# A copy of the first weights at another address, a fixed order for one chunk, and a prepared mean in a two-layer encoder

## The chip, the core and the metric

The kernel runs on one core of a Trainium2 chip. The core has a matmul engine (TensorE, PE in the profile; its weight loads stand apart as PEld), three engines for elementwise work (VectorE, DVE; ScalarE, ACT; GpSimd, POOL), a queue engine (SyncE, SP) and 16 DMA engines. Each engine runs its own instructions in order and waits for the others on semaphores. The metric is the device time of one execution in microseconds (us), the median over several runs of the same kernel.

## The reference

Two encoder layers on 256 tokens of width 2048, with 256 memory tokens beside them. In short:

```python
m = rms_norm(mem, mem_norm)
for i in range(2):
    n = rms_norm(h, attn_norm[i])
    # layer 0: 12 heads of 2-D neighbourhood attention with a bias
    # layer 1: 12 query heads on 4 key heads, normed q and k, rotary positions
    # both: 4 more heads that attend to the memory
    q, k, v, qm = split(n @ w_in[i])
    km, vm = split(m @ w_mem_kv[i])
    h = h + concatenate([mix(q, k, v), memory_attention(qm, km, vm)]) @ w_o[i]
    n = rms_norm(h, mlp_norm[i])
    h = h + square(relu(n @ w_up[i])) @ w_down[i]      # 2048 -> 8192 -> 2048
return rms_norm(h, final_norm)
```

All arrays are float32. The output is 256 x 2048.

## The kernel before

Every large product is made of three matmuls. A float32 operand is split into `hi` (rounded by ACT to the matmul's type) and `lo` (the rest, a subtraction on DVE), and the product sums hi x hi, hi x lo and lo x hi. The function `split` (L399) does this for weights, which come in chunks of 128 x 2048 (1 MB a DMA on SP, tile `raw`), a chunk in two halves (`hf` 0 and 1) of 1024 columns.

Matmuls come in two forms. In the S form (`products`, L306) the weights are the stationary operand, 128 x 128, and the activations stream past them, 256 columns at a time. The projections of queries and keys (`ps_s`) and the up projection of the MLP (`ps_u`) are of this form. In the M form (`m_products`, L289) the activations are stationary and 512 columns of weights stream: values, the output projection and the plain part of the down projection (`ps_m`). The down projection of the other parts (`p1` to `p7`, L913 to L925) also streams 512 columns.

The work is a list of grains (`Grain`, L115) that `run_all` (L343) goes through. A grain has a run (its matmuls) and earlier stages: load, pre and prep (the splits), each called a given number of grains ahead. A scheduler then orders the instructions of each engine from what they depend on and when it believes them ready. Where the program wants an order of its own it says so: `pin` keeps an instruction in the program's order, and `tc.issue_after(x)` lets nothing inside it be issued before `x`. `past` (L702) uses two such rules, one for an ACT and one for a DVE instruction.

Several constants (L39 to L52) shift tiles by some bytes within their rooms, so that what streams and what is loaded as stationary lie at chosen addresses: `STILL_AT` for the S form's weights, `MOVING_AT`, `LAST_AT`, `U_AT`. `ENTRY_AT` (160 bytes) belongs to `entered_half` (L267): where an S chunk follows an M chunk, the first 128 columns of `lo` are put at an address of their own (`Entered`, L101), and the first three matmuls of that chunk begin with `lo`. The tiles `hi` and `lo` are 64 elements longer than a half, which is the room for the shifts.

The MLP's up projection runs in 8 parts of 8 chunks (`up_grains`, L809). Part 0 stands before the down projection; each chunk of parts 1 to 7 stands between two grains of the part before it: down first, up (48 matmuls of 256 columns), down second. That makes a step of some 10 us. ACT and DVE split the weights of the next step meanwhile.

In layer 1 the output projection follows attention closely. `add_o` (L775) puts the chunks of output blocks 0 and 1 into one order, in which the chunk `late`, whose heads are the last to be ready, comes last for both blocks. The last two chunks are marked `behind` (L786): the split of their second half waits for the softmax of the newest head (`box["sm"]`, an exp on ACT and a product on DVE), and the very last chunk multiplies in `last_but_one` (L255), in which the products of its second quarter wait for the newest `av` product. The heads run as three stages each, `attend`, `attend2` (transposes, then the split into `pT`) and `attend3` (`av`, then the split into `cat`), set by `attention` (L492) at given distances in grains.

The end of the kernel is `finish` (L1099), once for each half of the tokens: it adds the last 512 columns to `h`, squares them on ACT, sums the four parts of the mean square, takes the root on POOL (`rstd_of`, L404), scales, and stores.

Of the kernel before, what the change touches and what calls it, by code (L numbers as in the profile page):

```python
# [14 lines left out]
ALU = mybir.AluOpType  # L15
# [36 lines left out]
ENTRY_AT = 160  # L52
# [13 lines left out]
class Work:  # L66


    def __init__(self, kind, src, acts, first, begins, last, start, done):
        self.kind, self.src, self.acts = kind, src, acts  # L70
        self.first, self.begins, self.last, self.start, self.done = first, begins, last, start, done
        self.early = self.behind = False
# [48 lines left out]
def encoder_kernel(ctx: ExitStack, tc: tile.TileContext, t: dict, out: bass.AP):  # L121
# [79 lines left out]
    def halves_of(w):  # L201
# [53 lines left out]
    def last_but_one(w, hi, lo):  # L255

        for i in range(NT):
            m_products(w, w.first, 1, i, hi, lo, False, False)
        with tc.issue_after(box["av"].ins):
            for i in range(NT):  # L260
                m_products(w, w.first + 1, 1, i, hi[:, 512:], lo[:, 512:], False, False)

    def new_half(kind):
        s = slice(STILL_AT // 4, STILL_AT // 4 + HALF) if kind == "S" else slice(0, HALF)
        return tuple(at.ring.tile([P, HALF + 64], F32R, tag=n, bufs=4, name=n)[:, s] for n in ("hi", "lo"))
# [23 lines left out]
    def m_products(w, k0, nk, i, hi, lo, begins, ends, keep_order=False):  # L289

        acts = w.acts
        for j in range(nk):
# [7 lines left out]
            nc.tensor.matmul(w.ps[i], al, hi[:, s], start=False, stop=sp)  # L300
# [5 lines left out]
    def products(ps, acts, k0, nk, hi, lo, keep_order=False):  # L306

        for j in range(nk):
# [7 lines left out]
            for n, (x, part) in enumerate(parts):  # L316
                ins = nc.tensor.matmul(ps, x[:, s], acts[:, k, part], start=k == n == 0,  # L317
# [129 lines left out]
    def attend(qT, kT, bias=None):  # L447
# [16 lines left out]
        for s in range(NT):  # L464
            exp = nc.scalar.activation(sc[:, s, :], src[:, s, :], AF.Exp, bias=nm[:, s : s + 1],
                                       accum_out=sm[:, s : s + 1])
        rs = small.tile([P, NT], F32, tag="rs", name="rs")
        nc.vector.reciprocal(rs, sm)
        for s in range(NT):
            times = nc.vector.tensor_scalar(sc[:, s, :], sc[:, s, :], rs[:, s : s + 1], None, op0=ALU.mult)  # L470
        box["sm"] = exp, times
        return sc

    def attend2(sc):
# [6 lines left out]
        split(pT[:, 0], pT[:, 1], pt)  # L481
        return pT
# [9 lines left out]
    def attention(jobs, at, gap=1, lag=1, rest=0):  # L492


        def step(n, job, prev):
# [3 lines left out]
            elif n == 1:  # L499
                res = attend2(prev)  # L500
            else:
                return attend3(prev, v, head, cat)
# [272 lines left out]
    def add_o(layer):  # L775
        first, second, third, late = 3, 0, 1, 2
        for n in (0, 2):
# [7 lines left out]
            if layer and n == 0:  # L785
                plan[-1].behind = plan[-2].behind = True  # L786
# [22 lines left out]
    def up_grains(layer, part, m):  # L809
# [5 lines left out]
        def prep(hf):  # L815
# [10 lines left out]
            else:  # L826
                own[hf] = half_of_side(own["raw"], hf)

        def run(hf):
# [14 lines left out]
            products(own["ps"], box["hT" if part else "hT0"], hf * (KT // 2), KT // 2, *own.pop(hf), keep_order=part > 0)  # L844
# [254 lines left out]
    def finish(w, i):  # L1099
# [4 lines left out]
        sum_squares(3, i, 3)  # L1104
        s = small.tile([P, 1], F32, tag="ss0", name="ss_f")
        nc.vector.tensor_reduce(s, ssq[3][:, i, :], axis=AX.X, op=ALU.add)
        r = rstd_of(s, D, "fin")
        nc.vector.scalar_tensor_tensor(hs, hs, r, box["gf"][:, last], op0=ALU.mult, op1=ALU.mult)
        for a in range(3):
            p = h[:, i, a * 512 : (a + 1) * 512]  # L1110
            if a == 2:
                nc.vector.tensor_scalar(p, p, r, None, op0=ALU.mult)
            else:
                nc.scalar.activation(p, p, AF.Copy, scale=r)
        for a in (0, 3, 2, 1):
            c = slice(a * 512, (a + 1) * 512)
            (nc.sync if a > 1 else nc.scalar).dma_start(out[i * P : (i + 1) * P, c], h[:, i, c])
# [74 lines left out]
    def b_q_done(blk):  # L1192
        def f(w):
# [5 lines left out]
                       for j, kv in enumerate(kvs)], 1, 2, 3, blk // 2)  # L1199
# [167 lines left out]
```

## Time and profile before

| | us |
|---|---|
| median of 3 runs (lowest to highest) | 2038.89 (2038.46 to 2041.59) |
| the profiled execution | 2037.55 |
| its span, first to last instruction | 2035.8 |
| PE busy | 2022.8 |
| DVE busy | 1661.9 |
| ACT busy | 1246.9 |
| POOL busy | 119.2 |

DMA moved 433.83 MB, 213 GB/s on the mean. A row of a group gives the line, the engine, the operation, out<-in, the shapes and the count; then busy time in us, the mean duration of one in ns, and the engine's idle time before them with what ended it. A row of a single line's view has least, median and greatest duration in ns, and the first and last start in us. A timeline row begins with start and length in us and ends with the idle time before it. Matmuls overlap in the array, so their durations are longer than the time from one start to the next.

### The profile page before, as it was taken

The numbers are of one execution on the slowest core, as the hardware profiler recorded it, in microseconds if no ns is written. First come the engines' busy times: TensorE is split into PE (matmuls) and PEld (weight loads), VectorE is DVE, ScalarE is ACT, GpSimd is POOL, SyncE is SP. The second block draws the span as 40 slices with busy tenths as digits, with TensorE's granted clock in tenths as the row PEclk, the third lists the DMA queues.
The fourth block names the chain that finished last, engine by engine and source line by source line (L and its number), as shares of the span: only waits on it lengthen the run. The fifth ranks groups of instructions, "written<-read, shape, count | busy, mean of one in ns | idle before, by whom it ended". The sixth has DMA issues, their size and how long they took to land.

```text
span 2035.8 us, 32561 instructions
## 1 busy us (share of the span) xinstructions
PE 2022.8 (99%) x13112; PEld 1836.5 (90%) x13112; DVE 1661.9 (82%) x2031; ACT 1246.9 (61%) x1618; POOL 119.2 (6%) x144
## 2 busy tenths in 40 slices
PE   9999999999999999999999999999999999999998
PEld 8999999899999999999988888789999999999996
DVE  6766666658998999989996667657999989999996
ACT  6655454556666666666655557656666666666664
POOL 0000000000000000000000001000000000000000
PEclk9999999999999999999999999999999999999999
DMA  7755555637777777777765544537777777777763
GB/s 286 303 185 182 178 176 179 242 135 233 233 233 233 226 235 231 221 238 222 237 203 212 179 170 145 186 130 238 232 233 233 219 244 217 233 238 222 240 218 126
DMA packets 77303, 433.83 MB, mean 213 GB/s; under 512 B 8672, under 2 KB 10336, under 8 KB 29664
## 3 DMA queue, kind: packets, MB, share of 16 engines
q1 hardware_dynamic: 59616, 399.21, 56.4%
q0 software_dynamic: 16816, 31.46, 8.9%
q8 instruction: 102, 1.67, 0.3%
q10 hardware_dynamic: 720, 1.09, 0.1%
q14 instruction: 49, 0.40, 0.1%
HBM read 398.17 MB, written 4.19 MB: 198 GB/s over the span
## 4 chain that ended last, share of the span: by engine, by line
PE 96%; DVE 1%; DMA 1%; ACT 1%; issue 1%; SPq 0%; POOLq 0%; POOL 0%; DVEq 0%; ACTq 0%
PE ps_u L317 33%; PE ps_s L317 10%; PE p L924 9%; PE p L922 9%; PE p L925 9%; PE ps_m L296 8%; PE ps_m L299 8%; PE ps_m L300 8%; PE pt_a L479 1%; PE pt_n L419 1%; DMA b<-b 0%; PE av L488 0%; PE av L489 0%; PE sc_ps L453 0%; PE sc_ps L452 0%
## 5 line engine op out<-in xcount | busy, mean ns | idle before, releaser
L317 PE MATMUL ps_u<-hT,uh 128*128 128x256 f32 x3892 | 673.8, 277 | 0.0
L317 PEld LDWEIGHTS ps_u<-hT,uh 128*128 128x128 f32 x3892 | 595.8, 188 | 9.1
L317 PE MATMUL ps_u<-hT,ul 128*128 128x256 f32 x1940 | 536.3, 277 | 0.0
L401 ACT ACTIVATE uh<-raw_U 128x1024 fp32r<-128x1024 f32 x266 | 282.3, 1062 | 274.1 <-PE ps_u L317 248.4
L402 DVE TENSOR_TENSOR lo<-raw,hi 128x1024 fp32r<-128x1024 f32 (+1 forms) x215 | 255.5, 1194 | 147.2 <-ACT hi L401 145.1
L317 PEld LDWEIGHTS ps_u<-hT,ul 128*128 128x128 f32 x1940 | 364.6, 188 | 0.0
L402 DVE TENSOR_TENSOR ul<-raw_U,uh 128x1024 fp32r<-128x1024 f32 x266 | 323.5, 1219 | 39.9 <-ACT uh L401 39.6
L401 ACT ACTIVATE hi<-raw 128x1024 fp32r<-128x1024 f32 (+1 forms) x215 | 222.5, 1039 | 199.4 <-PE ps_m L300 110.4
L401 ACT ACTIVATE bh<-b 128x2048 fp32r<-128x2048 f32 x112 | 215.3, 1922 | 117.8 <-PE p L925 90.0
L402 DVE TENSOR_TENSOR bl<-b,bh 128x2048 fp32r<-128x2048 f32 x112 | 256.1, 2287 | 19.1 <-ACT bh L401 19.1
L402 DVE TENSOR_TENSOR tl<-t,th 128x1536 fp32r<-128x1536 f32 x112 | 196.5, 1754 | 39.4 <-ACT th L401 38.4
L401 ACT ACTIVATE th<-t 128x1536 fp32r<-128x1536 f32 x112 | 166.7, 1489 | 38.6 <-PE p L925 38.6
L924 PE MATMUL p<-bl,a_s 128*128 128x512 f32 x448 | 174.6, 390 | 0.2
L925 PE MATMUL p<-bh,a_s 128*128 128x512 f32 x448 | 174.5, 390 | 0.0
L922 PE MATMUL p<-bh,a_s 128*128 128x512 f32 x448 | 174.4, 389 | 0.0
L894 POOL DMA_DIRECT2D b<-b x112 | 97.1, 867 | 1137.3 <-DVE t L893 997.8
L317 PE MATMUL ps_s<-nT,hi 128*128 128x256 f32 x896 | 157.8, 279 | 0.0
L317 PEld LDWEIGHTS ps_s<-nT,hi 128*128 128x128 f32 x896 | 136.4, 188 | 0.2
L922 PE MATMUL p<-th,a_s 128*128 128x512 f32 x336 | 131.4, 391 | 0.0
L924 PE MATMUL p<-tl,a_s 128*128 128x512 f32 x336 | 131.2, 390 | 0.0
L925 PE MATMUL p<-th,a_s 128*128 128x512 f32 x336 | 130.7, 389 | 0.0
L317 PE MATMUL ps_s<-nT,lo 128*128 128x256 f32 x448 | 125.1, 279 | 0.0
(250 smaller groups left out, 3492.9 us busy)
## 6 DMA issues: line engine op xcount, KB each, us to landing
raw_U<-in_w_up SPq DMA_DIRECT2D x128, 1024.0 KB, 5.0
b<-in_w_pair SPq DMA_DIRECT2D x112, 1024.0 KB, 5.1
raw<-in_w_o SPq DMA_DIRECT2D x32, 1024.0 KB, 5.0
b<-b POOLq DMA_DIRECT2D x112, 256.0 KB, 3.4
raw<-in_w_b SPq DMA_DIRECT2D x21, 1024.0 KB, 5.0
raw<-in_w_av SPq DMA_DIRECT2D x12, 1024.0 KB, 5.0
raw<-in_w_aq SPq DMA_DIRECT2D x12, 1024.0 KB, 5.0
raw<-in_w_ak SPq DMA_DIRECT2D x12, 1024.0 KB, 4.9
```

What stands on the lines that cost most here:

```text
L296: first = nc.tensor.matmul(w.ps[i], ah, hi[:, s], start=st, stop=False)
L299: nc.tensor.matmul(w.ps[i], ah, lo[:, s], start=False, stop=False)
L300: nc.tensor.matmul(w.ps[i], al, hi[:, s], start=False, stop=sp)
L317: ins = nc.tensor.matmul(ps, x[:, s], acts[:, k, part], start=k == n == 0, stop=k == KT - 1 and n == 2)
L401: first = nc.scalar.activation(dst_hi, src, AF.Copy)
L402: return first, nc.vector.tensor_tensor(dst_lo, src, dst_hi.bitcast(F32), op=ALU.subtract)
L419: nc.tensor.transpose(pt[:, b, i * P : (i + 1) * P], src(i, k), ident)
L479: nc.tensor.transpose(pt[:, k, i * P : (i + 1) * P], sc[:, s, k * P : (k + 1) * P], ident)
L894: nc.gpsimd.dma_start(b[:, 3, :], b[:, 1, :], accum_op=ALU.add)
L922: ins = nc.tensor.matmul(ps, a[:, 0, ai, :], hi[:, s], start=begins, stop=False)
L924: nc.tensor.matmul(ps, a[:, 0, ai, :], lo[:, s], start=False, stop=False)
L925: nc.tensor.matmul(ps, a[:, 1, ai, :], hi[:, s], start=False, stop=ends)
```

## The change

There are four parts.

1. For each chunk of the up projection in parts 1 to 7, ACT makes a copy of the first 128 columns of the raw weights, rounded like `hi`, in a room of its own (`u_0`, 384 bytes into the tile `junk`). The first matmul of the chunk takes this copy as its stationary operand; the other 47 read what they read before.
2. `ENTRY_AT` goes from 160 to 416, and the `lo` tiles get 128 elements of room in place of 64.
3. The very last chunk of layer 1's first output blocks is multiplied in a fixed order (`late_products`): its first half as before, its second half not before the last product of the other block's late chunk. The order of the grains is changed so that the first halves of both late chunks stand ahead of the second halves (`order[-3], order[-2]` are exchanged). The split of a `behind` chunk's second half waits for the split of `pT` of the last or last but one head, in place of the softmax. The last `av` of a group of heads waits for the products of the late chunk's second quarter (`box["between"]`). The last head of the last group comes one grain later (`blk // 2 * 2`).
4. In `finish` the mean over the first three column blocks is prepared before the last one is there; the fourth is added in one instruction. ACT scales columns 0 to 255 and 256 to 767, DVE 768 to 1535. The stores are cut at the same columns, three on SP and one on ACT (before: two and two).

```diff
-ENTRY_AT = 160
+ENTRY_AT = 416
+
+LONGER = {"hi": 64, "lo": 128}
+
+COPY_AT = 384
...
             if w.behind and hf == 1:
 
                 tiles[hf] = new_half(w.kind)
-                past(lambda: split(*tiles[hf], src), box["sm"])
+                past(lambda: split(*tiles[hf], src), box["pT", NH - 1 if w.last_block else NH - 2])
...
-                if w.behind and w.last and hf == 0:
-                    last_but_one(w, hi, lo)
+                if w.behind and w.last_block:
+                    late_products(w, hf, hi, lo)
                     return
                 for i in range(NT):
-                    m_products(w, w.first + 2 * hf, 2, i, hi, lo, w.begins and hf == 0, w.last and hf == 1)
+                    box["late"] = m_products(w, w.first + 2 * hf, 2, i, hi, lo, w.begins and hf == 0,
+                                             w.last and hf == 1)
...
+    def late_products(w, hf, hi, lo):
+
+
+        if hf == 0:
             for i in range(NT):
-                m_products(w, w.first + 1, 1, i, hi[:, 512:], lo[:, 512:], False, False)
+                m_products(w, w.first, 1, i, hi, lo, False, False)
+            with tc.issue_after(box["av"].ins):
+                for i in range(NT):
+                    box["between"] = m_products(w, w.first + 1, 1, i, hi[:, 512:], lo[:, 512:], False, False)
+        else:
+            with tc.issue_after(box["late"].ins):
+                for i in range(NT):
+                    m_products(w, w.first + 2, 2, i, hi, lo, False, True)
...
-        lo = Entered(at.ring.tile([P, HALF + 64], F32R, tag="lo", bufs=4, name="lo"))
+        lo = Entered(at.ring.tile([P, HALF + LONGER["lo"]], F32R, tag="lo", bufs=4, name="lo"))
...
             for n, (x, part) in enumerate(parts):
-                ins = nc.tensor.matmul(ps, x[:, s], acts[:, k, part], start=k == n == 0,
+                x = first if n == j == 0 and first is not None else x[:, s]
+                ins = nc.tensor.matmul(ps, x, acts[:, k, part], start=k == n == 0,
                                        stop=k == KT - 1 and n == 2)
...
+            if isinstance(w, Work) and w.last_block:
+
+                order[-3], order[-2] = order[-2], order[-3]
...
-                return attend3(prev, v, head, cat)
+                if "between" not in box:
+                    return attend3(prev, v, head, cat)
+                with tc.issue_after(box.pop("between").ins):
+                    return attend3(prev, v, head, cat)
...
+            if part and hf == 0:
+
+                room = at.side.tile([P, 256], F32R, tag="junk", bufs=1, name="u_0")
+                own["first"] = room[:, COPY_AT // 4 :][:, :P]
+                nc.scalar.activation(own["first"], own["raw"][:, :P], AF.Copy)
...
         s = small.tile([P, 1], F32, tag="ss0", name="ss_f")
-        nc.vector.tensor_reduce(s, ssq[3][:, i, :], axis=AX.X, op=ALU.add)
-        r = rstd_of(s, D, "fin")
+        nc.vector.tensor_reduce(s, ssq[3][:, i, :3], axis=AX.X, op=ALU.add)
+        v = small.tile([P, 1], F32, tag="rs_v", name="fin_v")
+        nc.vector.tensor_scalar(v, s, 1.0 / D, EPS, op0=ALU.mult, op1=ALU.add)
+        m = small.tile([P, 1], F32, tag="ss0", name="ms_f")
+        nc.vector.scalar_tensor_tensor(m, ssq[3][:, i, 3:], 1.0 / D, v, op0=ALU.mult, op1=ALU.add)
+        r = small.tile([P, 1], F32, tag="rs_r", name="fin_r")
+        nc.gpsimd.tensor_tensor(r, m, mhalf[:, :1], op=ALU.pow)
...
+        p = [h[:, i, x:y] for x, y in ((0, 256), (256, 768), (768, D - 512))]
+        nc.scalar.activation(p[0], p[0], AF.Copy, scale=r)
+        nc.scalar.activation(p[1], p[1], AF.Copy, scale=r)
+        nc.vector.tensor_scalar(p[2], p[2], r, None, op0=ALU.mult)
+        for eng, x, y in ((nc.sync, 0, 256), (nc.sync, D - 512, D), (nc.scalar, 256, 768), (nc.sync, 768, D - 512)):
+            eng.dma_start(out[i * P : (i + 1) * P, x:y], h[:, i, x:y])
...
-                       for j, kv in enumerate(kvs)], 1, 2, 3, blk // 2)
+                       for j, kv in enumerate(kvs)], 1, 2, 3, blk // 2 * 2)
```

More of the change, by code (lines that the diff above doesn't have):

```diff
@@ L71, in __init__ @@
         self.first, self.begins, self.last, self.start, self.done = first, begins, last, start, done
-        self.early = self.behind = False
+        self.early = self.behind = self.last_block = False
 class Shifted:
@@ L299, in m_products, with products @@
             nc.tensor.matmul(w.ps[i], ah, lo[:, s], start=False, stop=False)
-            nc.tensor.matmul(w.ps[i], al, hi[:, s], start=False, stop=sp)
+            final = nc.tensor.matmul(w.ps[i], al, hi[:, s], start=False, stop=sp)
+        return final
     def s_products(w, k0, nk, hi, lo):
         products(w.ps, w.acts(), k0, nk, hi, lo)
-    def products(ps, acts, k0, nk, hi, lo, keep_order=False):
+    def products(ps, acts, k0, nk, hi, lo, keep_order=False, first=None):
         for j in range(nk):
@@ L469, in attend @@
         for s in range(NT):
[L470 to L471 removed]
+            nc.vector.tensor_scalar(sc[:, s, :], sc[:, s, :], rs[:, s : s + 1], None, op0=ALU.mult)
         return sc
@@ L480, in attend2 @@
         pT = at.work.tile([P, 2, NT, SEQ], F32R, tag="pT", name="pT")
-        split(pT[:, 0], pT[:, 1], pt)
-        return pT
+        return pT, split(pT[:, 0], pT[:, 1], pt)
     def attend3(pT, v, head, cat):
@@ L843, in run @@
                     own["ps"] = sum_of("up")[:, :SEQ]
-            products(own["ps"], box["hT" if part else "hT0"], hf * (KT // 2), KT // 2, *own.pop(hf), keep_order=part > 0)
+            products(own["ps"], box["hT" if part else "hT0"], hf * (KT // 2), KT // 2, *own.pop(hf), keep_order=part > 0,
+                     first=own.pop("first", None))
         def after():
```

23 lines of the change are left out of this document (5 added, 18 removed).

## The prediction

> **What bounds the kernel.** I read the page first, then groups by line in narrow windows, then the timeline where TensorE (PE) stands still.
>
> ```profile
> span 2035.8 us, 32561 instructions
> PE 2022.8 (99%) x13112; PEld 1836.5 (90%) x13112; DVE 1661.9 (82%) x2031; ACT 1246.9 (61%) x1618; POOL 119.2 (6%) x144
> ...
> PE 96%; DVE 1%; DMA 1%; ACT 1%; issue 1%; SPq 0%; POOLq 0%; POOL 0%; DVEq 0%; ACTq 0%
> PE ps_u L317 33%; PE ps_s L317 10%; PE p L924 9%; PE p L922 9%; PE p L925 9%; PE ps_m L296 8%; PE ps_m L299 8%; PE ps_m L300 8%; PE pt_a L479 1%; PE pt_n L419 1%; DMA b<-b 0%; PE av L488 0%; PE av L489 0%; PE sc_ps L453 0%; PE sc_ps L452 0%
> ```
>
> PE is busy 99% and is 96% of the chain that ended last. Time can come only from how fast matmuls follow each other, from the few stalls, and from the two ends. The profiled execution took 2037.55 us, its span and 1.75 us around it; the median of the runs shown is 1.34 us above it. The sum is made against 2037.55 and its difference applied to 2038.89.
>
> **Part 1, the copy for up runs.** The change's arithmetic is in addresses. I call "distance" the start of what the matmul before streams, less the start of the stationary operand loaded meanwhile, modulo 512 bytes; I worked it out from the tiles' addresses in the built programs. All 112 up runs of parts 1 to 7 (2 layers x 7 parts x 8 chunks) are entered at 160 before and 288 after. First and last of them, each its first five matmuls, and behind the first the rest of its run:
>
> ```profile
> L317 PE MATMUL ps_u<-hT,uh x4: 281/282/286, 485.3 to 485.8; 128*128 128x256 f32 x4
> L317 PE MATMUL ps_u<-hT,ul x1: 283/283/283, 485.5 to 485.5; 128*128 128x256 f32 x1
> ...
> L317 PE MATMUL ps_u<-hT,uh x26: 276/276/276, 486.0 to 490.2; 128*128 128x256 f32 x26
> L317 PE MATMUL ps_u<-hT,ul x12: 276/276/276, 486.2 to 490.0; 128*128 128x256 f32 x12
> ...
> L317 PE MATMUL ps_u<-hT,uh x4: 281/282/286, 1975.8 to 1976.2; 128*128 128x256 f32 x4
> L317 PE MATMUL ps_u<-hT,ul x1: 283/283/283, 1976.0 to 1976.0; 128*128 128x256 f32 x1
> ```
>
> The three numbers are least, median and greatest duration in ns. The same shape takes 276 ns in 38 matmuls and 281 to 286 in the first five: (281 + 2x282 + 286 + 283) - 5x276 = 34 ns over, in the first run as in the last. Is a longer duration time lost? At 276 the 38 start (490.2 - 486.0)/37 = 113.5 ns apart. The rows of the projections give the other pace:
>
> ```profile
> L317 PE MATMUL ps_s<-memT,hi x121: 281/281/281, 52.8 to 74.0; 128*128 128x256 f32 x121
> L317 PE MATMUL ps_s<-memT,lo x60: 281/281/281, 52.9 to 73.8; 128*128 128x256 f32 x60
> ...
> L317 PE MATMUL ps_s<-nT,hi x36: 276/276/276, 190.7 to 196.6; 128*128 128x256 f32 x36
> L317 PE MATMUL ps_s<-nT,hi x83: 280/281/281, 222.2 to 236.7; 128*128 128x256 f32 x83
> L317 PE MATMUL ps_s<-nT,hi x36: 281/281/281, 238.8 to 245.1; 128*128 128x256 f32 x36
> L317 PE MATMUL ps_s<-nT,hi x83: 280/281/281, 296.2 to 310.7; 128*128 128x256 f32 x83
> L317 PE MATMUL ps_s<-nT,hi x36: 281/281/285, 312.8 to 319.1; 128*128 128x256 f32 x36
> ```
>
> At 281 the 181 matmuls start (74.0 - 52.8)/180 = 117.8 ns apart. So 5 ns of duration are about 4.5 ns of path, and there are two lasting paces at the same shape. How a run is entered seems to decide which. Entries near the distances that matter, the first an up run entered at 416 out of a projection, the next two out of a transpose at 480 and 224:
>
> ```profile
> L317 PE MATMUL ps_u<-hT,uh x4: 281/282/286, 437.6 to 438.1; 128*128 128x256 f32 x4
> ...
> L317 PE MATMUL ps_u<-hT,uh x5: 281/281/282, 439.9 to 440.6; 128*128 128x256 f32 x5
> ...
> L317 PE MATMUL ps_u<-hT,uh x5: 276/276/369, 441.3 to 442.1; 128*128 128x256 f32 x5
> L317 PE MATMUL ps_u<-hT,ul x3: 276/276/281, 441.5 to 442.2; 128*128 128x256 f32 x3
> ...
> L317 PE MATMUL ps_s<-nT,hi x4: 276/276/276, 148.3 to 148.9; 128*128 128x256 f32 x4
> ```
>
> Entered at 480 (439.7 us) the stretch stays at 281; entered at 224 (441.3 us) it runs at 276 after one matmul of 281. The lone entry at 288, out of an attention matmul at 148.3 us, is at 276 from the start. Entries at 32 out of 512-column matmuls are the slow rows at 52.8, 222.2 and 296.2; one at 32 out of an attention matmul is the fast row at 190.7, so the distance is not all. On the whole 480 and 32, close to 0, end in the slow pace, 224 and 288, close to 256, in the fast one. The trace has no entry at 288 out of a 512-column matmul; its price lies between all 34 ns gained and, as after 32, a whole run of 48 at the slow pace (48 x 4.5 - 34 = 180 ns lost). I take the row it is nearest to, 224 with one slow matmul: 34 - 5 = 29 ns, x112 = **-3.2 us**.
>
> The copy itself is one ACT instruction of 128 columns a run, 112 in all:
>
> ```profile
> L401 ACT ACTIVATE kT<-k_s 128x256 fp32r<-128x256 f32 x12 | 4.8, 402 | 0.0
> ...
> 508.63 1.06 ACT L401 ACTIVATE uh<-raw_U 128x1024 fp32r<-128x1024 f32 x1 [0.72 <-PE ps_u L317]
> 511.36 1.06 ACT L401 ACTIVATE uh<-raw_U 128x1024 fp32r<-128x1024 f32 x1 [1.66 <-PE ps_u L317]
> ```
>
> From 402 ns for 256 columns and 1060 for 1024, 128 cost some 290 ns by a straight line. It stands on ACT between the two splits of a chunk, where ACT sits idle 1.66 us waiting for PE, so it costs nothing; without that cover it would delay the next split by 0.29 us a run. Its room holds one copy, so it must wait until the run before has read it; the split ahead of it on ACT already waits for a later matmul of that run (the 0.72), so no wait is added.
>
> **Part 2, the projections' entry.** Five entries out of 512-column matmuls go from 32 to 288. Behind them the slow pace holds for 192, 32, 128 and 128 matmuls, and for 54 more in each of two groups (the rows above): 588 x 4.5 ns = 2.65 us. Bounds: nothing, if the pace does not follow the entry, and all of it; below nothing I see no row, as the pace is already the slow one. Attention breaks some stretches early: I take **-2.4 us**. The longer `lo` tiles only move addresses.
>
> **Part 3, the late chunk.** Around layer 1's first output projection PE stands still, each time for DVE:
>
> ```profile
> 1300.71 2.94 ACT L401 ACTIVATE hi<-raw 128x1024 fp32r<-128x1024 f32 x3
> 1301.80 3.50 DVE L402 TENSOR_TENSOR lo<-raw,hi 128x1024 fp32r<-128x1024 f32 x3
> 1302.76 0.73 PE L296 MATMUL ps_m<-hi,cat 128*128 128x512 f32 x2
> 1304.21 0.50 PE L299 MATMUL ps_m<-lo,cat 128*128 128x512 f32 x1 [0.72 <-DVE lo L402]
> 1305.25 0.28 PE L487 MATMUL av<-pT,vb 128*128 128x256 f32 x1
> 1306.50 0.28 PE L489 MATMUL av<-pT,vb 128*128 128x256 f32 x1
> ...
> 1314.83 1.07 PE L300 MATMUL ps_m<-hi,cat 128*128 128x512 f32 x4
> 1315.41 1.23 DVE L402 TENSOR_TENSOR ul<-raw_U,uh 128x1024 fp32r<-128x1024 f32 x1 [2.60 <-ACT uh L401]
> 1316.55 1.28 DVE L749 TENSOR_TENSOR h<-ps_m,h 128x512 f32<-128x512 f32 x2
> 1317.29 0.50 PE L296 MATMUL ps_m<-hi,cat 128*128 128x512 f32 x1 [1.40 <-DVE h L749]
> ```
>
> A 512-column matmul takes 0.23 us here, a 256-column one 0.12. Two matmuls fill 1302.76 to 1304.21: 1.0 lost. Three `av` fill 1305.25 to 1306.50 and need 0.36: 0.9 lost. Four from 1314.83 need 0.91, the next is at 1317.29: 1.55 lost, and its slow first matmul adds 0.1. In all 3.55.
> After the change DVE has the four adds to `h` (L749), which free PE's sums, ahead of the splits `ul` that wait for up weights: the 1.65 goes. The chunks of the last block are prepared in another order, so the three splits in a row (hi on ACT, lo on DVE) stand apart: one comes before the softmax, and a second half is split behind pT's own split where it stood behind the softmax. The rules that fix PE's order add no semaphore, PE being in order anyway. SP loads one chunk of `w_o` ahead of one of `w_up`, which is needed only after this whole projection. What is late next: `cat` of the last two heads, queued on ACT and DVE behind two splits each (1.0 and 1.2 us), with the forced late products behind it on PE. Laying the new order out with these durations, PE waits some 0.6 and 0.3 us there. So 1.9 becomes 0.9, and the part gives **-2.65 us**; bounds -3.55 and, if the `cat` waits eat what the splits give back, -0.5.
>
> **Part 4, the last columns.**
>
> ```profile
> 2028.54 0.16 DVE L1106 TENSOR_REDUCE ss_f<-ssq 128x1 f32<-128x4 f32 x1 [0.79 <-ACT sq L691]
> 2028.73 0.15 DVE L408 TENSOR_SCALAR fin_v<-ss_f 128x1 f32<-128x1 f32 x1
> 2029.55 1.33 ACT L1114 ACTIVATE h<-h,fin_r 128x512 f32<-128x512 f32 x2 [1.04 <-POOL fin_r L410]
> 2030.30 0.95 ACTq L1117 DMA_DIRECT2D out<-h  x2
> ...
> GB/s 410 379 62 0 0 0 0 0 0 0 0 0 0 0 0 72 358 440 379 440 379 430 369 440 379 440 379 430 297 10 0 0 0 0 0 0 0 0 0 0
> ```
>
> One small DVE step leaves the chain (2028.54 to 2028.73: 0.19), and the first store waits for 256 columns (0.40) in place of 512 (0.67): 0.27. The stores then run at some 400 GB/s without a gap, so the end moves with their start: **-0.45 us**; 0.5 at most, and 0.1 if the last store, whose 768 columns DVE finishes little sooner than ACT its last 512 now, ends the stream.
>
> **Sum.** -3.2 - 2.4 - 2.65 - 0.45 = -8.7: 2028.85 for the profiled execution, 2030.2 for the median. PE stays the bound (DVE has 82%), so I expect nothing given back.
>
> **Rivals.** (a) Addresses do not matter to PE: the 34 ns come from the change of width, 512 to 256 columns, and the pace from something else. For it: the up run entered at 416 (its row above) starts as slowly as those at 160. Against it: 480 and 224 above, the same tiles, 1.6 us apart. Parts 1 and 2 then give nothing: 2038.89 - 3.1 = 2035.8.
> The Trainium skill, "TensorE: Matmul & The Clock Gate", section "Step-by-step: what each phase is for", says that loading the next weights takes no read bandwidth from the running matmul. By that rule (a) holds; the trace, 276 against 281 ns at one shape, speaks against it.
> (b) Slower: distances repeat after 256 bytes, so 288 acts as 32. For it: 192 and 448 alternate inside every run without a trace, and 160 and 416 start alike. Against it: 224 and 480 differ. Then up runs fall into the slow pace: 180 ns x 112 = +20.2, part 2 nothing, with parts 3 and 4: +17.1, 2056. It decides for slower once a run loses over 64 ns ((4.1 + 3.1)/112), slow in some 22 of its 48 matmuls.
> (c) Only one of parts 1 and 2 pays, or part 3 pays half: 2032 to 2033.5.
>
> **Chances.** Forecast 0.55, its own range 2027.5 to 2032; (c) 0.17; (a) 0.13; (b) 0.12, other losses 0.03. The range runs from the sum of the best bounds (-3.8 - 2.65 - 3.55 - 0.5 = -10.5, 2028.4, less a little for the runs' spread) to past (a): 2027 to 2037. A measurement tells 0.2%, some 4 us: faster 0.70 (forecast and (c)), same 0.16 ((a) and edges), slower 0.14.
>
> **What would show it.** Right: first five matmuls of up runs at 276 to 281 ns; `ps_s` at 276 at 53 to 74 us and 222 to 237 us; no wait for `h` L749 near 1317 us; first store some 0.45 us sooner behind the last matmul. Wrong: up runs at 281 throughout (b), or five slow ones as before (a); waits for `cat` near 1309 us over 1 us.

## The result and the profile after

| | before | after |
|---|---|---|
| median, us | 2038.89 (7 runs, 2038.16 to 2041.84) | 2032.73 (7 runs, 2032.33 to 2033.11) |
| profiled execution | 2037.55 | 2032.67 |
| its span | 2035.8 | 2030.9 |

The ratio of the times is 0.9966, 95% interval 0.9955 to 0.9978: 6.2 us less by the medians, 4.9 by the two profiles. The forecast was 8.7 less (2030.2). The time lies inside the range, but where the third rival put it, that only one of parts 1 and 2 pays (2032 to 2033.5).

From the page of the changed kernel, the lines that answer to those of before (lines of the file have moved: L317 is now L330, L401 L417, L402 L418, L749 L766):

```profile
span 2030.9 us, 32731 instructions
PE 2018.9 (99%) x13112; PEld 1832.5 (90%) x13112; DVE 1663.5 (82%) x2033; ACT 1268.3 (62%) x1730; POOL 119.3 (6%) x144
...
L330 PEld LDWEIGHTS ps_u<-hT,uh 128*128 128x128 f32 x3780 | 573.8, 188 | 5.4
```

PE runs the same 13112 matmuls in the same places of its sequence, with few swaps, so that the start of matmul number n can be set against the start of number n before. The differences of those starts say where the time went:

| stretch (times before) | gain, us |
|---|---|
| start to 437.6, all projections and attention of layer 0 | -0.1 |
| 437.6 to 485.1, part 0 of the up products, layer 0 | -0.7 |
| 485.1 to 1055.1, the 56 up runs of layer 0 | +1.5 |
| 1055.1 to 1299.8 | 0.0 |
| 1299.8 to 1317.6, the late chunk | +3.0 |
| 1317.6 to 1363.6 | 0.0 |
| 1363.6 to 1411.2, part 0, layer 1 | -0.7 |
| 1411.2 to 1981.2, the 56 up runs of layer 1 | +1.5 |
| 1981.2 to the last matmul | 0.0 |
| last matmul to the end | +0.4 |

The first and the last up run that take the copy (`u`), in the view of one tile, with least, median and greatest duration in ns:

```profile
L330 PE MATMUL ps_u<-hT,u x1: 275/275/275, 486.0 to 486.0; 128*128 128x256 f32 x1
L330 PE MATMUL ps_u<-hT,uh x27: 276/276/276, 486.4 to 490.8; 128*128 128x256 f32 x27
...
L330 PE MATMUL ps_u<-hT,uh x2: 276/276/276, 1971.4 to 1971.6; 128*128 128x256 f32 x2
L330 PE MATMUL ps_u<-hT,u x1: 275/275/275, 1971.3 to 1971.3; 128*128 128x256 f32 x1
```

The five matmuls of 281 to 286 ns are gone; a run is at 276 from its first one. The projections, same view, have not moved:

```profile
L330 PE MATMUL ps_s<-memT,hi x122: 281/281/281, 52.7 to 74.1; 128*128 128x256 f32 x122
L330 PE MATMUL ps_s<-nT,hi x85: 280/281/281, 222.1 to 236.8; 128*128 128x256 f32 x85
L330 PE MATMUL ps_s<-nT,hi x84: 281/281/281, 296.1 to 310.7; 128*128 128x256 f32 x84
```

PE's waits after, in the groups by cause (in total, times, longest, us):

```profile
PE ps_u L330 <- DVE u_tl L418: 1.5, 2, 0.9
PE idle L193 <- POOL mhalf L187: 1.0, 1, 1.0
PE ps_s L330 <- ACT memT L443: 0.3, 1, 0.3
PE ps_m L311 <- DVE cat L418: 0.3, 1, 0.3
```

The 1.4 us for `h` has left this list. The first row is new at this length: it is the -0.7 in each layer. In both layers the second to last half of part 0 (`u_th`, `u_tl`) stands on ACT behind the split `bh`, which waits for a transfer. That row before and after, in the timeline:

```profile
471.72 1.92 ACT L401 ACTIVATE bh<-b 128x2048 fp32r<-128x2048 f32 x1 [2.09 <-DMA b<-b]
473.54 1.04 ACT L401 ACTIVATE u_th<-raw_U 128x1024 fp32r<-128x1024 f32 x1
```

```profile
472.34 1.92 ACT L417 ACTIVATE bh<-b 128x2048 fp32r<-128x2048 f32 x1 [2.62 <-DMA b<-b]
474.16 1.04 ACT L417 ACTIVATE u_th<-raw_U 128x1024 fp32r<-128x1024 f32 x1
```

All work ahead of it stands 0.07 to 0.08 us later than before, and the transfer of `b` landed 0.62 later; PE then stood 0.83 us in place of 0.28, and 1.03 in place of 0.37 in layer 1.

The late chunk after, in the timeline:

```profile
1300.88 1.05 ACT L417 ACTIVATE hi<-raw 128x1024 fp32r<-128x1024 f32 x1
1304.60 0.60 ACT L417 ACTIVATE pT<-pt_a 128x512 fp32r<-128x512 f32 x1 [2.67 <-PE pt_a L494]
1305.10 2.00 ACT L417 ACTIVATE hi<-raw 128x1024 fp32r<-128x1024 f32 x2
1306.99 0.37 ACT L417 ACTIVATE cat<-av 128x256 fp32r<-128x256 f32 x1
...
1306.18 2.36 DVE L418 TENSOR_TENSOR lo<-raw,hi 128x1024 fp32r<-128x1024 f32 x2 [0.26 <-ACT hi L417]
1308.46 0.42 DVE L418 TENSOR_TENSOR cat<-av,cat 128x256 fp32r<-128x256 f32 x1
1310.93 1.29 DVE L766 TENSOR_TENSOR h<-ps_m,h 128x512 f32<-128x512 f32 x2 [0.59 <-PE ps_m L311]
...
1308.22 0.40 PE L310 MATMUL ps_m<-lo,cat 128*128 128x512 f32 x1
1308.93 0.50 PE L311 MATMUL ps_m<-hi,cat 128*128 128x512 f32 x1 [0.31 <-DVE cat L418]
1313.70 0.39 PE L307 MATMUL ps_m<-hi,cat 128*128 128x512 f32 x1
```

The adds to `h` run at 1310.93, well ahead of the matmul at 1313.70 that needs their sums. The gaps at `lo` and `av` are gone. One wait has come: between 1308.22 and 1308.93 lie 0.71 us where 0.23 are needed, and PE waits for `cat`, whose second half DVE makes only at 1308.46, behind two splits `lo`, which stand behind two splits `hi`, which stand behind a `pT` for which ACT sat idle 2.67 us.

The end:

```profile
2022.04 0.39 PE L311 MATMUL ps_m<-h_p,a_p 128*128 128x512 f32 x1
...
2024.01 0.16 DVE L1134 SCALAR_TENSOR_TENSOR ms_f<-ssq,fin_v 128x1 f32<-128x1 f32 x1 [0.79 <-ACT sq L708]
2024.84 0.51 ACT L1139 ACTIVATE h<-h,fin_r 128x256 f32<-128x256 f32 x1 [0.86 <-POOL fin_r L1136]
2025.37 1.31 SPq L1143 DMA_DIRECT2D out<-h  x3
```

From the last matmul's start to the first store are 3.33 us; before, with its last matmul at 2026.58 and its store at 2030.30, 3.72. Of these 0.39 the end of the span kept 0.36.

### The profile page after: what moved, and what is told of

Read it like the earlier page. It is cut to its first block, busy times and chain, and to the rows that moved or that the text cites. A ratio compares the mean times of both kernels' runs of the same rounds, so it can differ in the third digit from the quotient of the medians.

```text
span 2030.9 us, 32731 instructions
## 1 busy us (share of the span) xinstructions
PE 2018.9 (99%) x13112; PEld 1832.5 (90%) x13112; DVE 1663.5 (82%) x2033; ACT 1268.3 (62%) x1730; POOL 119.3 (6%) x144
## 4 chain that ended last, share of the span: by engine, by line
PE 96%; DVE 1%; DMA 1%; issue 1%; ACT 1%; SPq 0%; POOLq 0%; DVEq 0%; POOL 0%; ACTq 0%
PE ps_u L330 32%; PE ps_s L330 10%; PE p L947 9%; PE p L948 9%; PE p L945 9%; PE ps_m L311 8%; PE ps_m L307 8%; PE ps_m L310 8%; PE pt_a L494 1%; DMA b<-b 1%; PE pt_n L435 1%; PE sc_ps L469 0%; PE sc_ps L468 0%; PE sc_ps L470 0%; PE av L501 0%
## 5 line engine op out<-in xcount | busy, mean ns | idle before, releaser
L330 PE MATMUL ps_u<-hT,uh 128*128 128x256 f32 x3780 | 657.6, 276 | 0.0
L330 PEld LDWEIGHTS ps_u<-hT,uh 128*128 128x128 f32 x3780 | 573.8, 188 | 5.4
L330 PE MATMUL ps_u<-hT,ul 128*128 128x256 f32 x1940 | 535.6, 276 | 0.0
L417 ACT ACTIVATE uh<-raw_U 128x1024 fp32r<-128x1024 f32 x266 | 282.2, 1062 | 248.1 <-PE ps_u L330 230.1
L418 DVE TENSOR_TENSOR lo<-raw,hi 128x1024 fp32r<-128x1024 f32 (+1 forms) x215 | 255.9, 1194 | 144.8 <-ACT hi L417 142.7
L330 PEld LDWEIGHTS ps_u<-hT,ul 128*128 128x128 f32 x1940 | 364.0, 188 | 0.0
L418 DVE TENSOR_TENSOR ul<-raw_U,uh 128x1024 fp32r<-128x1024 f32 x266 | 323.9, 1220 | 37.5 <-ACT uh L417 37.3
L417 ACT ACTIVATE hi<-raw 128x1024 fp32r<-128x1024 f32 (+1 forms) x215 | 222.4, 1039 | 199.8 <-PE ps_m L311 110.7
L417 ACT ACTIVATE bh<-b 128x2048 fp32r<-128x2048 f32 x112 | 215.3, 1922 | 106.4 <-PE p L948 90.7
L418 DVE TENSOR_TENSOR bl<-b,bh 128x2048 fp32r<-128x2048 f32 x112 | 256.2, 2288 | 18.9 <-ACT bh L417 18.8
L418 DVE TENSOR_TENSOR tl<-t,th 128x1536 fp32r<-128x1536 f32 x112 | 196.6, 1756 | 39.9 <-ACT th L417 39.3
L417 ACT ACTIVATE th<-t 128x1536 fp32r<-128x1536 f32 x112 | 166.8, 1489 | 38.6 <-PE p L948 38.2
L330 PE MATMUL ps_s<-nT,hi 128*128 128x256 f32 x896 | 157.8, 279 | 0.0
L330 PEld LDWEIGHTS ps_s<-nT,hi 128*128 128x128 f32 x896 | 136.4, 188 | 0.2
L330 PE MATMUL ps_s<-nT,lo 128*128 128x256 f32 x448 | 125.1, 279 | 0.0
```

The lines of the kernel that those rows point to most:

```text
L330: ins = nc.tensor.matmul(ps, x, acts[:, k, part], start=k == n == 0, stop=k == KT - 1 and n == 2)
L417: first = nc.scalar.activation(dst_hi, src, AF.Copy)
L418: return first, nc.vector.tensor_tensor(dst_lo, src, dst_hi.bitcast(F32), op=ALU.subtract)
```

## Experiments

Two questions were open: why the same distance, 288, helped up runs and not projections, and whether the new stalls in part 0 belong to the change. Losses are counted so: from the start of the last 512-column matmul to the start of the 25th matmul of the run behind it, less 226.7 ns and 24 x 113.33 ns, which is what the fast pace takes. Before, the 112 up runs entered at 160 out of a down product lost 33 to 34 ns so; after, at 288, they lose 7 to 11, the mean 7.6.

In every experiment here that varies a distance, the stationary operand was moved and what streams stayed where it was (in the built programs every 512-column matmul ahead of an entry streams from 128 modulo 256). So the maps show what the stationary operand's address does; that it is the distance to the stream which counts, and not that address by itself, is a way of counting and is not shown.

### Sixteen distances for the copy, five for the projections

```diff
-                own["first"] = room[:, COPY_AT // 4 :][:, :P]
+                at_byte = 32 * ((5 * part + m) % 16)
+                own["first"] = room[:, at_byte // 4 :][:, :P]
...
+ENTRIES = __import__("itertools").cycle([32, 288, 128, 384, 448])
...
+        entry = next(ENTRIES)
...
-        self.first = room[:, (STILL_AT + ENTRY_AT) // 4 + HALF - P :][:, :P]
+        self.first = room[:, (STILL_AT + entry) // 4 + HALF - P :][:, :P]
```

> The copy for up runs is made in all 112, but its place differs from run to run, so that the entry's distance takes all sixteen multiples of 32 in turn (4 to 10 runs each); the five entries of the projections take 160, 416, 64, 320 and 256. Theory D (the distance at the entry decides, near 256 good, near 0 bad): runs entered at 192 to 352 lose at most 10 ns over their first six matmuls, those at 416 to 96 lose 30 ns or more or stay slow (118 ns apart, some 180 ns a run); of the projections those at 320 and 256 are fast (113 apart) and 416 and 64 slow. Theory C (the copy itself, a first stationary operand in a tile of its own, does it, its address nothing): all sixteen are like 288, 113 apart from the first. Theory M (distances repeat after 256): 32 is like 288, 160 like 416. Theory P (projections stay slow whatever their entry): all five at 118. The span is that of the changed kernel, plus up to some 10 us if half of the runs turn slow under D.

Measured: the span was 2044.1 us. The loss of up runs in ns, the mean over the runs of each distance:

| distance | 0 | 32 | 64 | 96 | 128 | 160 | 192 | 224 |
|---|---|---|---|---|---|---|---|---|
| loss | 7.5 | 7.4 | 104.1 | 115.9 | 124.4 | 34.3 | 104.4 | 115.9 |
| distance | 256 | 288 | 320 | 352 | 384 | 416 | 448 | 480 |
| loss | 7.4 | 7.7 | 104.2 | 115.8 | 124.3 | 34.4 | 104.1 | 115.9 |

The two rows are the same within 1 ns: distances repeat after 256 bytes. Rows of the trace of this kernel, at 0, 448, 416 and 32:

```profile
L334 PE MATMUL ps_u<-hT,uh x31: 276/276/281, 484.4 to 489.5; 128*128 128x256 f32 x31
L334 PE MATMUL ps_u<-hT,uh x30: 281/281/281, 505.1 to 510.2; 128*128 128x256 f32 x30
L334 PE MATMUL ps_u<-hT,uh x31: 276/276/286, 515.5 to 520.6; 128*128 128x256 f32 x31
L334 PE MATMUL ps_u<-hT,uh x28: 276/276/276, 702.3 to 707.0; 128*128 128x256 f32 x28
```

For up runs theory M holds. Theory D falls (0 is good, 192 is bad), and C falls too: a copy at 160 loses what the run without a copy lost, and a copy at ten of the other distances loses three times as much. Of the projections the entries at 160 (at 53 us) and 256 (at 295 us) are fast, 64, 320 and 416 slow:

```profile
L334 PE MATMUL ps_s<-memT,hi x124: 276/276/280, 53.1 to 73.8; 128*128 128x256 f32 x124
L334 PE MATMUL ps_s<-nT,hi x84: 281/281/283, 222.1 to 236.7; 128*128 128x256 f32 x84
L334 PE MATMUL ps_s<-nT,hi x86: 276/276/282, 295.4 to 309.7; 128*128 128x256 f32 x86
```

So P falls: a projection can be brought to the fast pace. It was not, because 32 and 288 are the same distance.

### Five more distances for the projections

> The changed kernel, only the projections' five entries moved, to the distances 192, 128, 480, 352 and 96. Theory D: 192 and 352 are fast behind the entry (276 ns, 113 apart), 480 and 96 slow (281 ns, 118 apart), 128 between. Theory P: all five slow, and the span that of the changed kernel within 0.3 us; under D some 0.6 us less for each of the entries that holds the fast pace for 128 matmuls. The stall before the second half in which part 0 of the up products ends (0.83 us near 476.8 us and 1.03 us near 1402.8 in the changed kernel, 0.28 and 0.37 before): if it is chance of a transfer it takes another length here; if the change brings it, it is 0.8 and 1.0 again, as nothing here differs around it.

(The entries' places are 0, 64, 224, 352 and 96; else the changed kernel.) Measured: one run of 2029.8 us, the span 2028.0, 2.9 us under that of the changed kernel. Fast behind 192, 128, 352 and 96, slow behind 480. Two of the rows, entered at 352 and 96, which are one distance:

```profile
L334 PE MATMUL ps_s<-nT,hi x86: 276/276/282, 221.9 to 236.2; 128*128 128x256 f32 x86
L334 PE MATMUL ps_s<-nT,hi x86: 276/276/282, 294.9 to 309.2; 128*128 128x256 f32 x86
```

D falls here as well: 96 and 128 were to be bad or between, and are good. The stalls of part 0 were 0.56 and 0.30 us, with the same instructions around them as in the changed kernel (0.83 and 1.03).

### The changed kernel without parts 1 and 2

```diff
-ENTRY_AT = 416
-LONGER = {"hi": 64, "lo": 128}
+ENTRY_AT = 160
+LONGER = {"hi": 64, "lo": 64}
...
-            if part and hf == 0:
+            if False:
```

> The changed kernel without parts 1 and 2: no copy, the projections entered at 32 again; late chunk and last columns as changed. By the traces parts 3 and 4 alone gain some 3.3 us (2.96 in the late chunk, 0.36 at the end): 2035.5. The first five matmuls of up runs at 281 to 286 ns again. Theory S1 (the copies cause the longer stalls before the last half of part 0, 0.55 and 0.66 us more): stalls back at 0.28 and 0.37. Theory S2 (chance of a transfer, or part 3 or the tiles' addresses): not tied to the copy, any length.

Measured: 2034.72 us (10 runs, 2034.11 to 2035.33) against 2038.45 for the kernel before on that chip, ratio 0.9978, interval 0.9969 to 0.9987. Parts 3 and 4 are worth 3.7 us by the medians, not 3.3. In the trace the late chunk takes 14.85 us, as in the changed kernel (17.81 before, from its matmul at 1299.8 to the one at 1317.6). Stalls: 0.41 and 0.29.

### The changed kernel without part 3

```diff
-                past(lambda: split(*tiles[hf], src), box["pT", NH - 1 if w.last_block else NH - 2])
+                past(lambda: split(*tiles[hf], src), box["sm"])
...
-                order[-3], order[-2] = order[-2], order[-3]
...
-                    late_products(w, hf, hi, lo)
+                    last_but_one(w, hi, lo)
```

> The changed kernel without part 3: the late chunk of layer 1 as before, the copy, the projections' entry and the last columns as changed. If the trace of the changed kernel is read rightly, it loses 2.96 us against the changed kernel: 2035.7; a wait of 1.4 us for the adds to h and the gaps at lo and av are back. Rival: half of it was given by other parts (the earlier arrival, other addresses), and it loses only some 1.5 us. The stalls before the last half of part 0 as in the expectation for the kernel without parts 1 and 2: with S1 0.8 and 1.0 us, with S2 any length.

Measured: 2035.80 us, 10 runs that spread from 2034.43 to 2040.26. The first theory holds by the medians: 3.1 us above the changed kernel's 2032.73, which was not run beside it. The spread came as a surprise, and the timeline of its late chunk tells of it:

```profile
1314.45 2.00 ACT L407 ACTIVATE uh<-raw_U 128x1024 fp32r<-128x1024 f32 x2 [3.61 <-DMA raw_U<-in_w_up]
1315.54 1.23 DVE L408 TENSOR_TENSOR ul<-raw_U,uh 128x1024 fp32r<-128x1024 f32 x1 [3.45 <-ACT uh L407]
1316.68 1.28 DVE L754 TENSOR_TENSOR h<-ps_m,h 128x512 f32<-128x512 f32 x2
```

ACT waited 3.61 us here for the up weights to land, 2.76 in the first profile of before. DVE splits them ahead of the adds to `h`, so PE's wait for `h` is as long as that transfer is late: PE stood 1.56 us over its need there in the first profile of before, 2.41 here. Stalls of part 0: 0.72 and 0.29.

### All projections entered at 256

```diff
-ENTRY_AT = 416
+ENTRY_AT = 448
```

> The changed kernel with one number changed: the projections' first stationary operand 32 bytes further, so that all five are entered at 256. Theory R (distances repeat after 256 bytes; for projections 0, 96, 128 and 192 lead to the fast pace, 32, 64 and 224 to the slow one, as the two maps show): all five run at 113 apart from the first matmul, 588 matmuls x 4.5 ns = 2.65 us less than the changed kernel: 2030.1, and 2029 if the stalls before the last half of part 0 are short as in the kernel with the second map. Theory V (the good entry of the map at 256 belongs to that one place, the last projection): only that entry is fast, some 0.6 us less: 2032.1.

Measured: 2030.47 us (5 runs, 2029.91 to 2032.42), before on that chip 2039.57, ratio 0.9955, interval 0.9942 to 0.9969. Four of the five entries are fast, the one at 53 us is slow:

```profile
L330 PE MATMUL ps_s<-memT,hi x126: 280/281/283, 53.0 to 74.9; 128*128 128x256 f32 x126
L330 PE MATMUL ps_s<-nT,hi x86: 276/276/282, 222.5 to 236.7; 128*128 128x256 f32 x86
```

Neither theory is whole: 256 is good at more than one place (V falls), but the first projection has a map of its own (fast at 96, 160 and 192, slow at 32 and 256). The traces show one thing that sets it apart: the two intervals between the last three 512-column matmuls ahead of it are some 229 and 234 ns, and the last such interval ahead of the other four is 226 or 227. That this is the cause is not shown.

### Steps of 8 bytes

> The changed kernel with the copies' places by turns at distances in steps of 8 bytes, 0 to 56, 144 to 176 and 232 to 248, and four of the projections' entries at 0, one at 256. Theory R: the projections' four entries at 0 are as fast as at 256 (113 apart). For up runs, if the pace goes by steps of 32 bytes, the loss over the fast pace is 7 ns at 0 to 24 and 32 to 56 alike; if it goes by finer steps, it changes in between, and the least loss may be below 7 ns. Were distances near 0 bad, as the prediction's pattern had it, all those from 232 to 24 would be slow: 104 ns or more lost in the first 24 matmuls.

(The copy's place and the entries' places differ from the changed kernel, nothing else.) Measured, loss of up runs in ns:

| distance | 232 | 240 | 248 | 0 | 8 | 16 | 24 | 32 | 40 | 48 | 56 | 144 | 152 | 160 | 168 | 176 |
|---|---|---|---|---|---|---|---|---|---|---|---|---|---|---|---|---|
| loss | 7.7 | 7.7 | 34.1 | 7.4 | 7.4 | 7.9 | 21.4 | 7.7 | 7.5 | 109.2 | 27.4 | 110.9 | 110.9 | 34.4 | 104.1 | 110.8 |

The map changes within 8 bytes and follows no order of nearness; no place is below 7.4. The four projections entered at 0 are fast, like the last four at 256 in the kernel above.

### The distance inside the run

```diff
-                own[hf] = half_of_side(own["raw"], hf)
+                own[hf] = half_of_side(own["raw"], hf, 32 * ((5 * part + m) % 8) if part and hf == 0 else 0)
```

> The changed kernel; the copy stays at distance 288 in all up runs, but the first half of each run's other stationary operands is shifted by 0 to 224 bytes in turn, so that the distance inside the run takes eight values while that of its entry stays. Theory E (the first matmul's distance alone decides the pace): all 112 runs at 113 apart. Theory I (the distance of the second matmul, or that inside the run, decides with it): some of the eight values are slow, 118 apart, over 100 ns lost in 24 matmuls; this would explain why 288 is good for an up run and bad for a projection. The projections' entries at 96, 64, 128, 160 and 192: by the maps 96, 128 and 192 fast, 64 slow, 160 open (fast once, slow once).

Measured: 2046.1 us. With the entry at 288 throughout, by the distance inside the run's first half (modulo 256; 14 runs each):

| inside | 0 | 32 | 64 | 96 | 128 | 160 | 192 | 224 |
|---|---|---|---|---|---|---|---|---|
| loss, ns | 157.5 | 89.3 | 7.7 | 167.7 | 129.1 | 102.6 | 8.2 | 120.8 |

Rows at 0, 192 and 64:

```profile
L334 PE MATMUL ps_u<-hT,uh x27: 281/283/284, 495.3 to 500.0; 128*128 128x256 f32 x27
L334 PE MATMUL ps_u<-hT,uh x29: 276/276/277, 516.3 to 521.0; 128*128 128x256 f32 x29
L334 PE MATMUL ps_u<-hT,uh x29: 275/276/277, 557.7 to 562.5; 128*128 128x256 f32 x29
```

Theory I holds: the first distance does not decide alone. Only 64 and 192 can run at 276; at the others the matmuls of a run follow each other unevenly, 113 to 125 ns apart, or, at 0, settle at 120. The kernel's up runs and projections are both at 192 inside (448 is the same), so this does not tell by itself why 32 is good for one and bad for the other. Of the projections' entries here, 96 was fast at 53 us, 64, 160 and 192 were slow, and 128, the entry of a run of seven, was fast from its fifth matmul on.

Put side by side, the traces of the maps narrow that question down. The first start behind the last 512-column matmul is the same for up runs and for the projections after the first one, within 1 ns: 227 ns at 0, 235 at 32, 226 at 64, 237 at 96, 232 at 128, 228 at 160, 226 at 192, 235 at 224. What differs comes behind it: at 32 the second matmul of an up run follows after 113 ns, that of a projection after 122. In the built programs the second stationary operand lies at 160 from that 512-column stream in an up run and at 192 in a projection (modulo 256). No run moved this alone in a projection, so it is a candidate and not a cause.

### The late halves behind the softmax again

> The changed kernel with one step of part 3 undone: the late halves are split behind the softmax again, not behind pT's split; order of the last block and of the late products as changed. If the gain of the late chunk lies in the order (the adds to h ahead of the up weights' splits), the chunk keeps 1.65 us or more of its 2.96 and this runs at most 1.3 us longer. If it lies in the splits' place, it loses over 1.5 us of them to gaps at lo and av.

(The `past` line and `box["sm"]` as before, all else as changed.) Measured: one run of 2031.0 us, span 2029.2. The late chunk takes 14.14 us, 0.71 less than with the changed kernel's step, a gain that the expectation did not foresee. Its timeline:

```profile
1299.49 2.00 ACT L417 ACTIVATE hi<-raw 128x1024 fp32r<-128x1024 f32 x2
1301.39 0.37 ACT L417 ACTIVATE cat<-av 128x256 fp32r<-128x256 f32 x1
...
1302.86 0.42 DVE L418 TENSOR_TENSOR cat<-av,cat 128x256 fp32r<-128x256 f32 x1
1303.19 1.28 DVE L418 TENSOR_TENSOR pT<-pt_a,pT 128x512 fp32r<-128x512 f32 x2
```

The splits fill the time that ACT otherwise sits idle ahead of `pT`, and no split is left between the last `av` and its `cat`. PE's gaps of over 60 ns in this chunk are 0.26 us in all; 1.03 in the changed kernel, 3.93 before. So the gain of part 3 lies in the order of the block, and its step from the softmax to `pT` costs 0.7.

### Both, the changed kernel again, and the kernel before again

The first takes the late halves behind the softmax, and `ENTRY_AT = 96`, with which all five projections are entered at 96.

> The changed kernel with two steps put otherwise: all five projections entered at 96 (three places have run fast there in the maps), and the late halves split behind the softmax as before the change. Theory R: all five entries fast from the second or third matmul, 588 x 4.5 ns less 13 ns each = 2.6 us below the kernel with the splits behind the softmax (2031.0, one run); in all 2028.4, some 4.3 us below the changed kernel. Rival: the late chunk's 0.7 us in that one run was chance of a transfer, as the other late chunks' waits vary; then 2029.1 or more.

> The changed kernel once more, unchanged, beside the other two on one chip. If the stalls before the last half of part 0 (0.83 and 1.03 us in its first profile) are chance of a transfer, this profile shows other lengths, and runs spread by up to 1.2 us; if the change brings them, they are 0.8 and 1.0 us again. The time: 2032.7 as before, within 0.6.

> The kernel before once more, unchanged. Its runs spread over 5 us (2037.2 to 2042.2) where those of the changed kernel spread over 1. If the old late chunk causes that, its waits around layer 1's first output projection (1.4 us for the adds to h in the first profile, 2.2 us in the kernel with the change's other parts alone) differ again by some tenths or more, while every other stretch agrees within 0.3 us. Otherwise the late chunk takes 17.8 us from its first transposes to the last wait as in the first profile.

Measured on one chip: 2028.17 us for both steps (5 runs, 2028.00 to 2028.32; ratio to before 0.9947, interval 0.9934 to 0.9961), 2031.84 for the changed kernel (2031.05 to 2032.14; 0.9964, 0.9952 to 0.9977; 0.9 under its first median), 2038.46 for before. Put otherwise the two steps give 3.7 us more, so that this kernel beats the changed one as well as the one before. All entries are fast, and no `h`, `lo`, `cat` or `av` is among PE's waits:

```profile
L330 PE MATMUL ps_s<-memT,hi x128: 276/276/277, 52.0 to 73.4; 128*128 128x256 f32 x128
L330 PE MATMUL ps_s<-nT,hi x86: 276/276/282, 220.6 to 234.9; 128*128 128x256 f32 x86
```

```profile
PE idle L193 <- POOL mhalf L187: 1.0, 1, 1.0
PE ps_u L330 <- DVE u_tl L418: 0.9, 2, 0.4
PE ps_s L330 <- ACT hi L417: 0.3, 1, 0.3
```

Its late chunk takes 14.16 us, so the 0.7 was no chance. The stalls of part 0, in us: changed kernel 0.83 and 1.03, again 0.45 and 0.86; before 0.28 and 0.37, again 0.30 and 0.64; both steps 0.60 and 0.60. One program gives lengths up to 0.4 apart. In all profiles, the three without the copy (six stalls) have a mean of 0.38, the ten with it (twenty) one of 0.57. That is too near the scatter to tell the two apart, and the first profiles of before and after lay near the two ends. The copies themselves cannot have lengthened the first profile's transfers: `bh` starts on `b` at 472.34 us in layer 0 and at 1394.79 in layer 1, and ACT makes the first copy of each layer only at 476.78 and 1399.23. Before's late chunk took 18.05 us this time (17.81), with 1.80 us in place of 1.56 lost at `h`.

## Why the prediction was right, and where it was wrong

**Part 1, -3.2 forecast, -2.97 measured** (1.50 and 1.47 in the two layers). The five slow matmuls went, and nothing of a run fell slow. What was not in the sum is the entry itself: the first matmul starts 235 ns after the last one of 512 columns, 228 before, so that some 26.6 ns a run are left of the 34. The reason given for 288 was wrong, though. "480 and 32, close to 0, end in the slow pace, 224 and 288, close to 256, in the fast one" does not hold: 288 acts as 32, and 32 as well as 0 is good for an up run. The result came out because the runs were at 160, which loses 34 ns, and 288 happens to be one of the four places of sixteen that lose 7; ten others would have lost 104 or more. The pattern that picked 288 did not make it one of the four, so that was luck. The copy adds no wait of its own to PE, as forecast.

**Part 2, -2.4 forecast, nothing measured.** This is the step that failed: the price was taken from the pattern of distances near 0 and near 256. It rested on entries at 480 and 224 behind transposes, with other things different between them: the first resumes an interrupted run with `ul`, the second begins a half with `uh`. The bound "nothing, if the pace does not follow the entry" was kept, but the right reason for nothing was not in it: the pace follows the entry, and the entry had not changed, since 416 and 160 differ by 256 bytes. The size was right: with 96 at all five entries the stretch from the first of them to the first up product (52 to 438 us in the changed kernel) takes 2.69 us less than in the changed kernel.

**Rival (b)** had the true premise, that distances repeat after 256 bytes, and drew from it that up runs would turn slow as the projections were. They are not slow at 32. What made the premise improbable in the text, "224 and 480 differ", came from those transposes again. **Rival (c)** is what happened: part 1 paid and part 2 did not.

**Rival (a)** falls most clearly. The kernel with sixteen distances has the instructions of the changed one and differs in addresses alone; its span is 13.2 us longer. The Trainium skill, "TensorE: Matmul & The Clock Gate", section "Step-by-step: what each phase is for", says that loading the next weights takes no read bandwidth from the running matmul; these runs sit badly with it, as the time between matmuls of one shape goes from 113 to 120 ns with the address of the stationary operand. They do not show whether it is read bandwidth that is lost.

**Part 3, -2.65 forecast, -2.95 measured.** The 1.65 at `h` went as forecast. At `cat` 0.9 was forecast as the new wait, and 0.59 came (0.48, and 0.11 in the slow matmul behind it). By the medians the part is worth 3.1: its other half, which no term of the sum had, is that before's wait hangs on a transfer of up weights that lands later in some executions than in others (ACT waited 2.76 and 3.00 us for it in two profiles of before, and 3.61 in the kernel without part 3).

**Part 4, -0.45 forecast, -0.36 measured.** The first store starts 0.39 sooner behind the last matmul. The forecast that the stores' end moves with their start held to within 0.03.

**"I expect nothing given back"** was wrong against the profile of before: part 0 gave back 0.55 and 0.66 us. The repeats show that this profile had short stalls and the other long ones. The parts make -2.97 - 2.95 - 0.36 = -6.28, close to the 6.16 between the medians; the profiles differ by 1.4 less, for the stalls. Sum and medians agree so well partly by luck, since the runs behind the medians hold late chunks and stalls of other lengths than the two profiles.

What stays open: why an entry at 32 is good for an up run and bad for a projection, what makes the first projection another case, and what makes the transfer ahead of part 0's stall land early or late. Weights are loaded well before their use (a load takes 188 ns, a matmul starts every 113), so more than one matmul's addresses may meet; this was not tried.

## What to carry to other kernels

A matmul's pace can depend on where its operands lie, and a pattern read from a few entries that differ in more than the address is not a map: vary the address alone over all places in one kernel, and read the paces from its trace. Before an address is moved by some bytes, ask for the period: a move by a whole period changes nothing. And a wait that hangs on the landing of a transfer is as long as that transfer is late; one profile shows one draw of it, the spread of the runs the rest.

## What was not expected of the hardware

- The time between two matmuls of one shape (128x128 stationary, 256 columns) depends on the address of the stationary operand, here counted as its distance from what streams, with a period of 256 bytes: sixteen distances at the entry gave 7 to 124 ns lost over 24 matmuls, equal for each pair 256 apart within 1 ns.
- The entry leaves a pace that lasts: 113.3 or 117.8 ns apart, for as long as 190 matmuls behind one first matmul. Of the eight distances tried inside a run, only 64 and 192 (modulo 256) kept the fast one.
- The map is finer than 32 bytes: 40 loses 7.5 ns, 48 loses 109, 56 loses 27.
- The same read-back of `b` let PE stand 0.28 to 1.03 us in different executions, with the same instructions ahead of it.
